# The low parts of one Strassen product first, at another place in SBUF

## The chip, the cores and the metric

The kernel runs on one core of a Trainium2 chip. The metric is the device time of one execution in microseconds, taken as the median of several runs. The times of the engines come from one execution that the hardware profiler recorded.

## What is computed

The reference is one decoder block over 512 positions of 1024 channels, all in float32. What matters here is its last part, the feed-forward layer:

```python
h = rmsnorm(x, norm2_g[l])
gu = h @ w_ffn_in[l]                       # 1024 -> 2 * 2816
g = causal_dwconv(gu[..., :D_FF], ffn_conv_w[l]) + ffn_conv_b[l]
x = x + (jax.nn.silu(g) * gu[..., D_FF:]) @ w_ffn_out[l]
```

Before it come a joint input projection, a gated convolution, an attention with compressed and selected blocks, and their merge. The change does not reach into those.

## The kernel before

**Two parts per number.** Every large product is computed with float32r operands. A float32 value is split into a high part (a rounded copy) and a low part (the rest), and a product is the sum of three: high weights by high data, high weights by low data, low weights by high data. `dense` (from L402) writes this out for a list of units, one unit per 128 input channels: first, for each unit, the two products with the high weights (L405, L406), which load the same weights twice; then, for each unit, the product with the low weights (L408). TensorE runs its matmuls in the order in which the program has them, each with a load of 128 x 128 weights ahead of it.

**The feed-forward layer.** `ff_strassen` (from L992) takes two tiles of 128 output channels at a time, f and f + 1, for f = 0, 2, ... 20. For each it computes two pairs: the gate (n = 0) and the up projection (n = 1). That makes 22 pairs. A pair is a 2 x 2 block product by Strassen's scheme in Winograd's form: 7 products in place of 8. `ff_forms` (from L898) builds the seven weight forms: the blocks a22, a11 and a12 as they are, and four sums of blocks, numbered 1 to 4. `ff_pair` (from L942) runs the seven products into four PSUM banks. Each product has 4 units, so 12 matmuls, with 256 columns of moving data from `xf_h` and `xf_l`; a pair has 84. The first product is always a22 with T4. For f = 0 the gate pair is written differently (`late`, the lines around L969 and L975): its first three units are issued while the data is still being made, and it does not call `dense` for its products.

**Down parts.** Between pairs, `between()` calls `down_part` (from L1013): a share of the last projection. For four tiles f at a time, two of the 8 output tiles are taken, each with 4 units of 512 columns; together 24 matmuls. From about 477 us of the span on, pair and down part take turns in a regular beat. Before that, parts and pairs are interleaved by the scheduler, which orders each engine's instructions with a simulation of the timeline.

**Where the weights lie.** The tiles of the weight forms are taken from the pool `pw` (L831 to L833) and, for a11 and a12, from the ring `wf`:

- `th` and `tl`, the high and the low part of a22, 2048 bytes per partition each, two buffers of each tag;
- `sh` and `sl`, the parts of the sums (three buffers each), `sf`, the sums before the split, and `p1`, all in `pw` behind them;
- `wh` and `wl`, the ring for a11 and a12.

Tiles get their place when their tag is first asked for. The line `pw.tile(..., name="th_", tag="th", bufs=2)` asks for `th` ahead of all others, and `gap_w`, 48 floats that nobody reads, follows it. So `th` begins 288 bytes past a multiple of 512, and `tl`, `sh`, `sl` and all that follow begin at 480. `wh` and `wl` begin at 480 too, and so does everything that the down parts read. The moving tiles `xf_h` and `xf_l` begin at 288. A weight block of one unit is 512 bytes per partition, so every unit of a tile starts at the same place within 512.

**How a22 is filled.** `dma_split` (L157 to L161): ScalarE writes the high part into `th` (L159) and the negated high part into `tl` (L160); then GpSimd issues a transfer that adds the raw weights to `tl` in place (L161). The other forms are split by ScalarE and VectorE (`split`, L152).

Of the kernel before, what the change touches and what calls it, by code (L numbers as in the profile page):

```python
# [11 lines left out]
F32 = mybir.dt.float32  # L12
F32R = mybir.dt.float32r
# [5 lines left out]
P = 128  # L19
D = 1024  # L20
# [62 lines left out]
def tile_block(ctx: ExitStack, tc: tile.TileContext, xT, pos, par, par2, w_tok, w_a3, w_gate, w_ao, w_bo, w_o,  # L83
               w_ff, w_dn, c_w1, out):
    nc = tc.nc
# [10 lines left out]
    def const(shape, name, dt=F32, pool=sb):  # L96
        return pool.tile(shape, dt, name=name, tag=name)
# [14 lines left out]
    def d_bank(name):  # L112
        return bank("d", name, 2)

    def s_bank(name):
        return bank("s", name, 3)

    def t_bank(name):
        return bank("t", name, 2)

    def o_bank(name):
        return bank("o", name, 1)
# [47 lines left out]
    def ring_w(src, name):  # L170
        raw = raw_tile(name)
        nc.sync.dma_start(raw, src)
        h, l = ring(name)
        split(h, l, raw)
        return h, l
# [223 lines left out]
    r1sq = const([P, S], "r1sq", F32, pb)  # L399
    nc.scalar.activation(r1sq, r1b, AF.Square)  # L400

    def dense(acc, units, first=True, last=True):  # L402

        for i, (wh, wl, xh, xl) in enumerate(units):
            nc.tensor.matmul(acc, wh, xh, start=first and i == 0, stop=False)  # L405
            nc.tensor.matmul(acc, wh, xl, start=False, stop=False)  # L406
        for i, (wh, wl, xh, xl) in enumerate(units):
            nc.tensor.matmul(acc, wl, xh, start=False, stop=last and i == len(units) - 1)  # L408

    def w_units(w, xh, xl, nk, k0=0, koff=0):  # L410
        wh, wl = w
        return [(wh[:, (koff + k) * P:(koff + k + 1) * P], wl[:, (koff + k) * P:(koff + k + 1) * P],
                 xh[:, k0 + k, :], xl[:, k0 + k, :]) for k in range(nk)]
# [15 lines left out]
    def compress_in(kv):  # L429
        w = load_w(w_a3[kv], D, f"kc{kv}")  # L430
        acc = d_bank(f"pkc{kv}")
        dense(acc, w_units(w, xg_h, xg_l, KD))
        kc2 = pp.tile([P, 8, G, NU_], F32, name=f"kcb{kv}", tag="kcb", bufs=1)

        pe = pe_sb[:, kv].rearrange("p (n r) -> p r n", r=8)
        for g in range(G):
            nc.gpsimd.tensor_copy(kc2[:, :, g, NC:].rearrange("p r (a n) -> p r a n", a=2),
                                  pe[:, :, None, :].to_broadcast([P, 8, 2, 2]))
            for j in range(2):
                nc.vector.tensor_tensor(  # L440
                    kc2[j * HD:(j + 1) * HD, :, g, 0:NC],
                    acc[g * HD:(g + 1) * HD, :].rearrange("p (n r two) -> p r n two", r=8, two=2)[:, :, :, j],
                    r1b[g * HD:(g + 1) * HD, :].rearrange("p (n r two) -> p r n two", r=8, two=2)[:, :, :, j], op=ALU.mult)
        hi, lo = (kc2s[:, :, i, kv] for i in range(2))
        nc.gpsimd.tensor_copy(hi, kc2)
        nc.vector.tensor_sub(lo, kc2, hi.bitcast(F32))
# [271 lines left out]
    def conv_tile(i):  # L718
        accs = []
        for j in (1, 2, 0):  # L720
            w = load_w(w_a3[2 + 3 * i + j], D, f"a{i}{j}", by="dma" if 3 * i + j > 1 else "vector")
            acc = d_bank(f"pa{i}{j}")
            dense(acc, w_units(w, xg_h, xg_l, KD))
            if j == 1:
                cs_ = f_tile(f"cs{i}")[:, 0:S]
                nc.vector.tensor_mul(cs_, acc, r1sq)
            elif j == 2:
                u = f_tile(f"u{i}")
                nc.gpsimd.memset(u[:, 0:2], 0.0)
                nc.vector.tensor_mul(u[:, 2:], acc, cs_)  # L730
                t = f_tile(f"ct{i}")[:, 0:S]
                causal_conv(t, u, par_sb[:, CAW + 3 * i:CAW + 3 * i + 3])
                nc.gpsimd.tensor_mul(t, t, r1b)
            else:
                nc.vector.tensor_mul(t, acc, t)
                nc.scalar.activation(ya_h[:, i, :], t, AF.Copy)
                nc.vector.tensor_sub(ya_l[:, i, :], t, ya_h[:, i, :].bitcast(F32))
# [3 lines left out]
    def gate_tile(j, t):  # L741
        w = load_w(w_gate[j], D, f"g{j}", by="pool")
        acc = d_bank(f"pg{j}")
        dense(acc, w_units(w, xg_h, xg_l, KD))
        nc.vector.tensor_mul(t, acc, r1b)
        nc.scalar.activation(t, t, AF.Tanh, scale=0.5)
# [57 lines left out]
    for i in range(4):  # L804
# [3 lines left out]
        w = ring_w(w_bo[i], f"bo{i}")  # L808
        for n, j in enumerate((2 * i, 2 * i + 1)):
            acc = t_bank(f"pmb{j}")  # L810
# [18 lines left out]
    xf_h = const([P, 4, 7, TH], "xf_h", F32R, px)  # L829
    xf_l = const([P, 4, 7, TH], "xf_l", F32R, px)  # L830
    pw = ctx.enter_context(tc.tile_pool(name="pw", bufs=1, side="left"))  # L831
    pw.tile([P, D // 2], F32R, name="th_", tag="th", bufs=2)
    const([P, 48], "gap_w", F32, pw)  # L833

    def x_forms(k, v):
        nc.vector.tensor_sub(v[:, T1:T3 + 1], v[:, 1:4:2], v[:, 0:2])
# [5 lines left out]
    for n, j in enumerate(O_ORDER):  # L842
        w = ring_w(w_o[j], f"o{j}")
        acc = d_bank(f"po_{j}")
        units = w_units(w, mix_h, mix_l, KD)
# [96 lines left out]
    def ff_pair(f, n, c, form, late=None):  # L942
        nm = f"{n}_{f}"
        b1, b26 = o_bank(f"p1{nm}"), t_bank(f"p26{nm}")
        b45, b37 = s_bank(f"p45{nm}"), s_bank(f"p37{nm}")
        lo, hi = slice(0, TH), slice(TH, S)

        def units(wf_, x, ks):
            wh, wl = form[wf_]
            return [(wh[:, k * P:(k + 1) * P], wl[:, k * P:(k + 1) * P], xf_h[:, k, x], xf_l[:, k, x]) for k in ks]  # L950

        def product(acc, wf_, x):
            dense(acc, units(wf_, x, range(4)))

        def sums(dst, bank, v):

            nc.vector.tensor_tensor(dst, bank.rearrange("p (a t) -> p a t", a=2), v[:, None, :].to_broadcast([P, 2, TH]),
                                    op=ALU.add)

        p1 = pw.tile([P, TH], F32, name=f"p1{nm}", tag="p1", bufs=1)  # L960
        c1, c2 = c[:, :, 0:TH], c[:, :, TH:]
        plan = [(b26, hi, 2, T2, True), (b37, hi, 3, T3, True), (b37, lo, 4, B22, False), (b45, hi, 1, T1, True),
                (b1, lo, "a11", B11, True), (b26, lo, "a12", B21, False), (b45, lo, "a22", T4, False)]
        if late is not None:

            for b, cols, wf_, x, opens in plan:
                for i, (wh, wl, xh, xl) in enumerate(units(wf_, x, range(3))):
                    for lhs, rhs, st in ((wh, xh, True), (wh, xl, False), (wl, xh, False)):
                        nc.tensor.matmul(b[:, cols], lhs, rhs, start=opens and st and i == 0, stop=False,  # L969
                                         skip_group_check=True)  # L970

            def product(acc, wf_, x):
                (wh, wl, xh, xl), = units(wf_, x, (3,))
                for lhs, rhs, last in ((wh, xh, False), (wh, xl, False), (wl, xh, True)):
                    nc.tensor.matmul(acc, lhs, rhs, start=False, stop=last, skip_group_check=True)  # L975

        product(b45[:, lo], "a22", T4)
        product(b1[:, lo], "a11", B11)
        nc.scalar.activation(p1, b1[:, lo], AF.Copy)
        product(b26[:, lo], "a12", B21)  # L980
        product(b26[:, hi], 2, T2)
        sums(c1, b26, p1)
        product(b37[:, hi], 3, T3)
        product(b37[:, lo], 4, B22)
        sums(c2, b37, c1[:, 1])
        product(b45[:, hi], 1, T1)
        sums(c[:, 1].rearrange("p (a t) -> p a t", a=2), b45, c2[:, 1])
        nc.vector.tensor_add(c2[:, 0], c2[:, 0], b45[:, hi])
# [121 lines left out]
```

## Time and profile before

| | |
|---|---|
| Median of 3 runs | 715.76 us (715.33 to 716.61) |
| The profiled execution: its time | 715.21 us |
| Its span, from the first to the last instruction | 713.5 us |
| Mean granted TensorE clock | 1.00 |
| Matmuls | 4285 |
| HBM read, written | 102.64 MB, 2.10 MB |

The span is shorter than the execution's time by what lies around it. The profile gives, for each engine, its busy time; for each group of equal instructions, the mean duration; and in the timeline, the start of each. A matmul's duration contains the way through the array, so two neighbours overlap: what a matmul costs in a row of matmuls is the distance between two starts, which is less than the duration. Groups in the timeline that are merged (x4) show the start of the first. The weight loads are a row of their own (PEld) and overlap the matmuls.

### The profile page before, as it was taken

The numbers are of one execution on the slowest core, as the hardware profiler recorded it, in microseconds if no ns is written. First come the engines' busy times: TensorE is split into PE (matmuls) and PEld (weight loads), VectorE is DVE, ScalarE is ACT, GpSimd is POOL, SyncE is SP. The second block draws the span as 40 slices with busy tenths as digits, with TensorE's granted clock in tenths as the row PEclk, the third lists the DMA queues.
The fourth block names the chain that finished last, engine by engine and source line by source line (L and its number), as shares of the span: only waits on it lengthen the run. The fifth ranks groups of instructions, "written<-read, shape, count | busy, mean of one in ns | idle before, by whom it ended". The sixth has DMA issues, their size and how long they took to land.

```text
span 713.5 us, 11375 instructions
## 1 busy us (share of the span) xinstructions
PE 708.3 (99%) x4285; PEld 633.5 (89%) x4285; DVE 534.8 (75%) x957; ACT 432.6 (61%) x722; POOL 182.4 (26%) x179
## 2 busy tenths in 40 slices
PE   9999999999999999999999999999999999999997
PEld 9999878888888888888889999899999999999986
DVE  6887886687566878365795899988787877878643
ACT  7535655977667776522676767666555765647440
POOL 4051422133433334433012220221211222111110
PEclk9999999999999999999999999999999999999999
DMA  7333687511121122336386797987978779785565
GB/s 274 97 95 119 172 181 162 135 60 59 60 69 51 60 76 73 118 128 197 94 197 137 174 236 196 226 209 183 213 183 211 175 185 206 185 198 105 123 142 149
DMA packets 41142, 105.47 MB, mean 148 GB/s; under 512 B 3968, under 2 KB 9216, under 8 KB 41088
## 3 DMA queue, kind: packets, MB, share of 16 engines
q1 hardware_dynamic: 26528, 70.41, 30.4%
q0 software_dynamic: 14272, 34.08, 27.6%
q8 instruction: 33, 0.54, 0.3%
q10 hardware_dynamic: 288, 0.26, 0.1%
q14 instruction: 21, 0.17, 0.1%
HBM read 102.64 MB, written 2.10 MB: 147 GB/s over the span
## 4 chain that ended last, share of the span: by engine, by line
PE 96%; DMA 2%; ACT 1%; issue 0%; DVE 0%; POOL 0%; ACTq 0%; POOLq 0%
PE p L406 9%; PE p L405 9%; PE p L408 9%; PE pdn L406 6%; PE pdn L405 6%; PE pdn L408 6%; PE pg L406 4%; PE pg L405 4%; PE pg L408 4%; PE pa L405 2%; PE pt L681 2%; PE pa L406 2%; PE pa L408 2%; PE po L405 2%; PE po L406 2%; PE po L408 2%
## 5 line engine op out<-in xcount | busy, mean ns | idle before, releaser
L406 PE MATMUL p<-xf_l,sh 128*128 128x256 f32 x336 | 80.6, 277 | 0.0
L405 PE MATMUL p<-xf_h,sh 128*128 128x256 f32 x336 | 80.5, 277 | 0.0
L153 ACT ACTIVATE sh<-s 128x1024 fp32r<-128x1024 f32 x44 | 46.2, 1057 | 38.2 <-PE p L406 24.7
L406 PE MATMUL pdn<-al,wh_d 128*128 128x512 f32 x176 | 68.8, 391 | 0.0
L405 PE MATMUL pdn<-ah,wh_d 128*128 128x512 f32 x176 | 68.5, 390 | 0.0
L405 PEld LDWEIGHTS p<-xf_h,sh 128*128 128x128 f32 x336 | 63.0, 188 | 0.1
L406 PEld LDWEIGHTS p<-xf_l,sh 128*128 128x128 f32 x336 | 63.0, 188 | 0.1
L161 POOL DMA_DIRECT2D wl_s<-in_w_ff_dram x22 | 19.5, 885 | 167.2 <-ACT wl_s L160 155.9
L154 DVE TENSOR_TENSOR sl<-s,sh 128x1024 fp32r<-128x1024 f32 x44 | 53.8, 1224 | 8.7 <-ACT sh L153 8.7
L159 ACT ACTIVATE wh_s<-wr_s 128x1024 fp32r<-128x1024 f32 x22 | 23.3, 1059 | 53.1 <-PE pdn L406 50.1
L408 PE MATMUL p<-xf_h,sl 128*128 128x256 f32 x336 | 51.5, 277 | 0.0
L136 POOL TENSOR_TENSOR wl_g<-wr_g,wh_g 128x1024 fp32r<-128x1024 f32 x16 | 38.4, 2401 | 50.7 <-ACT wh_g L134 25.4
L405 PE MATMUL pg<-xg_h,wh_g 128*128 128x512 f32 x128 | 50.7, 396 | 0.0
L406 PE MATMUL pg<-xg_l,wh_g 128*128 128x512 f32 x128 | 50.6, 395 | 0.0
L408 PE MATMUL pdn<-ah,wl_d 128*128 128x512 f32 x176 | 47.7, 389 | 0.0
L161 POOL DMA_DIRECT2D wl_d<-in_w_dn_dram x22 | 26.5, 1203 | 77.2 <-ACT wl_d L160 69.0
L1029 DVE TENSOR_TENSOR x<-x,pdn 128x512 f32<-128x512 f32 x48 | 33.0, 688 | 16.2 <-PE pdn L408 15.5
L408 PEld LDWEIGHTS p<-xf_h,sl 128*128 128x128 f32 x336 | 44.6, 188 | 0.2
L405 PE MATMUL p<-xf_h,wh_s 128*128 128x256 f32 x168 | 40.5, 276 | 0.0
L406 PE MATMUL p<-xf_l,wh_s 128*128 128x256 f32 x168 | 40.5, 276 | 0.0
L408 PEld LDWEIGHTS pdn<-ah,wl_d 128*128 128x128 f32 x176 | 33.0, 188 | 6.9
L406 PEld LDWEIGHTS pdn<-al,wh_d 128*128 128x128 f32 x176 | 33.0, 188 | 6.2
(359 smaller groups left out, 2123.1 us busy)
## 6 DMA issues: line engine op xcount, KB each, us to landing
wr_s<-in_w_ff_dram SPq DMA_DIRECT2D x44, 512.0 KB, 4.9
wl_s<-in_w_ff_dram POOLq DMA_DIRECT2D x22, 512.0 KB, 7.2
wr_d<-in_w_dn_dram SPq DMA_DIRECT2D x22, 512.0 KB, 7.0
wl_d<-in_w_dn_dram POOLq DMA_DIRECT2D x22, 512.0 KB, 8.2
wr_g<-in_w_gate_dram SPq DMA_DIRECT2D x16, 512.0 KB, 3.4
wr_a<-in_w_a_dram SPq DMA_DIRECT2D x12, 512.0 KB, 4.1
tl<-in_w_ff_dram POOLq DMA_DIRECT2D x22, 256.0 KB, 6.9
wl_a<-in_w_a_dram POOLq DMA_DIRECT2D x10, 512.0 KB, 7.9
```

Source lines behind the costliest of these rows:

```text
L136: e.tensor_sub(lo[:, 0:n], raw[:, 0:n], hi[:, 0:n].bitcast(F32))
L153: hi = nc.scalar.activation(h, v, AF.Copy)
L154: nc.vector.tensor_sub(l, v, h.bitcast(F32))
L159: nc.scalar.activation(h, raw, AF.Copy)
L161: nc.gpsimd.dma_start(l if dst is None else dst, src, accum_op=ALU.add)
L405: nc.tensor.matmul(acc, wh, xh, start=first and i == 0, stop=False)
L406: nc.tensor.matmul(acc, wh, xl, start=False, stop=False)
L408: nc.tensor.matmul(acc, wl, xh, start=False, stop=last and i == len(units) - 1)
L681: nc.tensor.transpose(pt[:, i * P:(i + 1) * P], e[:, i, (kt + k0) * P:(kt + k0 + 1) * P], ident)
L1029: nc.vector.tensor_add(xj, xj, acc)
```

## The change

`dense` gets an argument `low_first`. With it, the products with the low weights are issued ahead of those with the high ones; without it the order is as before. `ff_pair` sets it for the a22 product alone. In the pool `pw`, `tl` is now asked for ahead of the others, with a gap of 80 floats ahead of it and one of 96 floats behind it in place of 48; `th` gets its place behind that gap, where its tag is first asked for. So `tl` begins 96 bytes past a multiple of 512, and `th` at 480; all others keep their place within 512 and lie 512 bytes further on. The gate pair of f = 0 keeps its order, and has its tiles at the new places.

```diff
-    def dense(acc, units, first=True, last=True):
-
-        for i, (wh, wl, xh, xl) in enumerate(units):
-            nc.tensor.matmul(acc, wh, xh, start=first and i == 0, stop=False)
-            nc.tensor.matmul(acc, wh, xl, start=False, stop=False)
-        for i, (wh, wl, xh, xl) in enumerate(units):
-            nc.tensor.matmul(acc, wl, xh, start=False, stop=last and i == len(units) - 1)
+    def dense(acc, units, first=True, last=True, low_first=False):
+
+        products = [(wl, xh) for wh, wl, xh, xl in units]
+        highs = [(wh, x) for wh, wl, xh, xl in units for x in (xh, xl)]
+        products = products + highs if low_first else highs + products
+        for i, (w, x) in enumerate(products):
+            nc.tensor.matmul(acc, w, x, start=first and i == 0, stop=last and i == len(products) - 1)
...
     pw = ctx.enter_context(tc.tile_pool(name="pw", bufs=1, side="left"))
-    pw.tile([P, D // 2], F32R, name="th_", tag="th", bufs=2)
-    const([P, 48], "gap_w", F32, pw)
+
+    const([P, 80], "gap_v", F32, pw)
+    pw.tile([P, D // 2], F32R, name="tl_", tag="tl", bufs=2)
+    const([P, 96], "gap_w", F32, pw)
...
         def product(acc, wf_, x):
-            dense(acc, units(wf_, x, range(4)))
+            dense(acc, units(wf_, x, range(4)), low_first=wf_ == "a22")
```

## The prediction

> **What bounds the kernel.** I read the page from the top: the busy shares, the granted clock, then the chain that ended last.
>
> ```profile
> PE 708.3 (99%) x4285; PEld 633.5 (89%) x4285; DVE 534.8 (75%) x957; ACT 432.6 (61%) x722; POOL 182.4 (26%) x179
> PEclk9999999999999999999999999999999999999999
> PE 96%; DMA 2%; ACT 1%; issue 0%; DVE 0%; POOL 0%; ACTq 0%; POOLq 0%
> ```
>
> TensorE is busy 99% of the span at the full granted clock, and 96% of the chain that ended last is its own work. So only two things can move the time here: the distance from one matmul's start to the next one's, which I call the step, and a wait put in front of a matmul. The matmuls themselves stay the same in number and size, 12 for each a22 product.
>
> Next, the groups by line and shape, from 477 us to 693 us, where pairs and down parts alternate regularly (columns: line, engine, operation, output<-inputs, shapes, count | busy us, mean ns | idle before).
>
> ```profile
> L405 PE MATMUL p<-xf_h,sh 128*128 128x256 f32 x224 | 53.5, 276 | 0.0
> L406 PE MATMUL p<-xf_l,th 128*128 128x256 f32 x56 | 13.9, 282 | 0.0
> L405 PE MATMUL p<-xf_h,th 128*128 128x256 f32 x56 | 13.9, 281 | 0.0
> L408 PE MATMUL p<-xf_h,tl 128*128 128x256 f32 x56 | 8.6, 276 | 0.0
> ```
>
> All four rows are one shape, 256 columns. Only those whose weights lie in th, the high parts of a22, last 281 to 282 ns in place of 276. By the sizes in the code th is the one weight tile that does not start at 480 bytes past a multiple of 512: gap_w is 48 floats, so th lies 192 bytes lower than the rest, at 288. What a duration means for the step is read from the starts in the timeline. First an a22 product straight behind another pair:
>
> ```profile
> 406.84 0.28 PE L405 MATMUL p<-xf_h,th 128*128 128x256 f32 x1
> 406.96 0.28 PE L406 MATMUL p<-xf_l,th 128*128 128x256 f32 x1
> ...
> 407.80 0.28 PE L408 MATMUL p<-xf_h,tl 128*128 128x256 f32 x1
> ```
>
> Eight matmuls in 407.80 - 406.84 = 0.96 us: a step of 120 ns. Now one behind a down part, with the rest of its pair, up to the next down part:
>
> ```profile
> 491.67 1.07 PE L408 MATMUL pdn<-ah,wl_d 128*128 128x512 f32 x4
> 492.58 0.28 PE L405 MATMUL p<-xf_h,th 128*128 128x256 f32 x1
> ...
> 493.53 0.62 PE L408 MATMUL p<-xf_h,tl 128*128 128x256 f32 x4
> ...
> 502.14 0.39 PE L405 MATMUL pdn<-ah,wh_d 128*128 128x512 f32 x1
> ```
>
> From 492.58 to 493.53 the eight th matmuls take 0.95 us, 119 ns each. The other 76 of the pair (4 of tl, six products of 12) take 502.14 - 493.53 = 8.61 us, 113.3 ns each. The third place is the one that matters most. Here a down part was sorted into the a22 product, so that only one th matmul stands between the 512-column work and the rest of the pair:
>
> ```profile
> 462.34 0.84 PE L408 MATMUL pdn<-ah,wl_d 128*128 128x512 f32 x3
> 463.02 0.28 PE L406 MATMUL p<-xf_l,th 128*128 128x256 f32 x1
> 463.14 0.63 PE L408 MATMUL p<-xf_h,tl 128*128 128x256 f32 x4
> 463.61 0.28 PE L405 MATMUL p<-xf_h,wh_s 128*128 128x256 f32 x1
> ...
> 472.09 0.39 PE L405 MATMUL pdn<-ah,wh_d 128*128 128x512 f32 x1
> ```
>
> The same 76 matmuls, same weights' places, same moving tiles, take 472.09 - 463.14 = 8.95 us, 117.8 ns each. So TensorE has two rates for the same 256-column work, a short step of 113.3 ns and a long one of 117.8 ns, and keeps the one it has fallen into until something disturbs it. The next place shows what can disturb it:
>
> ```profile
> 396.57 1.10 PE L408 MATMUL p<-xf_h,sl 128*128 128x256 f32 x8
> 397.52 0.28 PE L405 MATMUL p<-xf_h,th 128*128 128x256 f32 x1
> ...
> 398.23 0.62 PE L408 MATMUL p<-xf_h,tl 128*128 128x256 f32 x4
> 398.68 0.28 PE L405 MATMUL p<-xf_h,wh_s 128*128 128x256 f32 x1
> ```
>
> Before the six th matmuls the step is long (397.52 - 396.57 = 0.95 for eight, 119 ns); after them it is short (398.68 - 398.23 = 0.45 for four, 113 ns). The reading I go by: th, out of line with the rest, costs some 6 ns a matmul, and in return a run of it brings TensorE from the long step back to the short one. A single th does not (463.02); six or eight do.
>
> **The change, part by part.** The order of the 12 matmuls becomes 4 of tl, then 8 of th. gap_v adds 80 floats (320 bytes) ahead of tl: 288 + 320 = 608, that is 96 past 512. gap_w grows to 96 floats, so th and all behind it begin at 288 + 704 = 992, which is 480 past 512. All other tiles move by 512 bytes and keep their place within 512.
>
> *High parts.* Eight th matmuls now have weights placed as all others are. If the short step holds, they take 8 x 113.3 = 907 ns. Now they take 950 behind a down part and 960 behind a pair. That takes off 43 ns or 53 ns.
>
> *Low parts.* Four tl matmuls move from 480 to 96. No row shows weights at 96. From below: they cost nothing more than now, 113.3 ns; no group of this shape has a shorter settled step, and I see no reason for one. From above: the settled step of th, 120 ns, 4 x 6.7 = 27 ns more. I take 11 ns, nearer to the low end, since behind a down part the full price isn't reached at once (119 against 120 ns). So 32 ns go per product behind a down part, 42 behind a pair.
>
> *How many.* The 22 products divide so: those behind a down part run from 492.58 to the last one,
>
> ```profile
> 671.99 1.07 PE L408 MATMUL pdn<-ah,wl_d 128*128 128x512 f32 x4
> 672.90 0.28 PE L405 MATMUL p<-xf_h,th 128*128 128x256 f32 x1
> ```
>
> With 15.03 us for 84 short steps and 24 of 512 columns (492.58 to the th of the next pair at 507.61), that is 13 of them, and one before at 477.55: 14 x 32 = 0.45 us. Two stand behind a pair, as at 406.84: 2 x 42 = 0.08 us. Six lie in the stretch from 380 to 477 us, mixed with other work; I give them 0 to 50 ns each, 0.1 us in all. Sum: about 0.6 us less. Against the profiled execution (715.21 us, of which 713.5 are the span and 1.7 lie around it) that is 714.6; the median of the runs is 0.55 us above that execution, so 715.76 - 0.6 = **715.2 us**.
>
> *The wait.* With its low parts first, a22 needs tl 0.95 us earlier. Tl comes through a transfer that GpSimd issues and that adds in place:
>
> ```profile
> 507.61 0.28 PE L405 MATMUL p<-xf_h,th 128*128 128x256 f32 x1
> 496.64 0.85 POOL L161 DMA_DIRECT2D tl<-in_w_ff_dram x1
> DMA to landing us min/median/max: 3.9/6.9/9.4
> ```
>
> The issue at 496.64 lands at the latest 9.4 us on, at 506.0, and the next a22 product begins at 507.61. Even if it were for that product, 1.6 us would be left; with two buffers per tile it is more likely meant for the one behind. So the wait is hidden, under the pair's and the down part's own matmuls. Without that cover TensorE would stand for up to 0.95 us per pair, with nothing else queued to go ahead of tl. DVE, ACT, GpSimd and SyncE get no instruction more, and none is moved on their queues.
>
> *A rule that speaks against it.* The row: th 281 to 282 ns, the others 276, and where the weights start is what the code sets apart. The Trainium skill, page "SBUF — State Buffer", section "Who interferes with whom", has TensorE read its moving operand and its weights through two independent ports and never wait on anyone, so the start within 512 bytes would be of no account and the change worth nothing. The trace disagrees as far as these rows go.
>
> **Rivals.** *The low parts at 96 do not restore the short step.* This is the one on the slow side. After 512-column work the place at 463.02 kept the long step for a whole pair, with weights at 480. If four matmuls at 96 are too few, or if 96 acts as 480 does, each of the 14 pairs behind a down part runs all its 84 matmuls at 117.8 ns: 9.89 us in place of 0.95 + 8.61 = 9.56, 0.33 us more. 14 x 0.33 = 4.6 us: 720.4 us. It decides in the first four steps of a pair. For it: the th run behind a down part needs more than one matmul, I have seen six and eight work, and 4 is half of what is there now. Against it: the moving tiles xf_h and xf_l begin at 288, so 480 lies 192 bytes ahead of them and 96 lies 192 bytes behind; th, right at their place, restores slowly, and a third place may do it sooner.
>
> *Place is of no account.* Then th is slow for what it is (its product, its bank, being first) and the change moves only the order: 715.8, give or take 0.2. For it: all th's lie in the pair's first product. Against it: the tl of that product has 276 ns.
>
> *The stretch from 380 to 477 us falls out otherwise.* There pairs and parts are interleaved and the long step is common:
>
> ```profile
> L405 PE MATMUL p<-xf_h,sh 128*128 128x256 f32 x112 | 27.0, 278 | 0.0
> ...
> L405 PE MATMUL p<-xf_h,sh 128*128 128x256 f32 x16 | 3.9, 279 | 0.0
> ```
>
> The first row is that stretch, 278 ns in the mean; the second is the long-step pair from 463.5 to 472.5 us alone, 279; the short step has 276. A pair that changes sides there is worth 0.34 us (76 x 4.5 ns). Three gained beside the forecast's 0.6: 714.2 us. Three lost: 716.2, which is within what counts as no change.
>
> **Chances.** A measurement of this kernel can tell about 0.2%, 1.4 us, from no change. The forecast, with its own range from 714.4 to 716.2 (a loss in the early stretch included): 0.52. Place of no account: 0.08. Both are within 0.2%: 0.60. The low parts fail to restore: 0.30. A gain past 1.4 us through the early stretch: 0.10. Faster 0.10, same 0.60, slower 0.30. Since the failing case has more than 2 in 10, the range must reach it: 714.2 to 720.8 us.
>
> **What would show it.** Right: the th groups at 276 ns, eight th in 0.91 us, the pair behind a down part still 8.6 us for 76 matmuls, and sh, sl and wh_s at 276 ns from 477 us on. If tl at 96 acts as th did, its groups show 280 to 282 ns. Wrong by the first rival: sh, sl and wh_s at 279 ns for whole pairs and 15.3 us instead of 15.03 from pair to pair. Wrong by the second: tl now has the 282 ns although th has 276, or th keeps 282 at its new place. A wait would show as idle time in front of the tl matmuls with GpSimd's transfer as its end.

## The result, and the profile after

| | before | after |
|---|---|---|
| Median of 4 runs each, side by side | 716.02 us (715.33 to 716.61) | 721.13 us (720.25 to 721.46) |
| Ratio after / before, 95% interval | | 1.0074 (1.0061 to 1.0086) |
| The profiled execution, its span | 715.21 us, 713.5 us | 720.25 us, 718.5 us |

The change costs 5.1 us, 0.7%. That is not the forecast of 715.2 us but its first rival, priced at 720.4; 721.13 us lies 0.3 us above even the upper end of the range, 720.8. The page of the kernel after, in the lines that were read of before (busy shares, clock, chain):

```profile
PE 713.2 (99%) x4285; PEld 637.9 (89%) x4285; DVE 534.8 (74%) x957; ACT 432.6 (60%) x722; POOL 182.2 (25%) x179
PEclk9999999999999999999999999999999999999999
PE 97%; DMA 2%; ACT 0%; DVE 0%; issue 0%; ACTq 0%
```

TensorE has as many matmuls as before, the same clock, and is the chain by itself. It is busy 4.9 us longer (713.2 against 708.3), nearly all of the 5.0 us by which the span grew. So nobody waits for anything new; the same matmuls follow each other more slowly. Which ones, the groups by line and shape from 477 to 698 us tell:

```profile
L408 PE MATMUL p<-xf_h,sh 128*128 128x256 f32 x224 | 55.2, 279 | 0.0
...
L408 PE MATMUL p<-xf_h,th 128*128 128x256 f32 x56 | 13.8, 279 | 0.0
...
L408 PE MATMUL p<-xf_h,tl 128*128 128x256 f32 x56 | 8.9, 282 | 0.0
```

th, now at 480, is no longer out of line: 279 ns, like sh. But sh, which keeps its place within 512 bytes, went from 276 to 279 ns, the mark of the long step, and so did all the rest of the pairs. The last column is the idle time ahead of the group: 0.0 ahead of tl, so the wait for its transfer is hidden. Now the starts in the timeline, from one down part over a pair to the next pair:

```profile
476.84 1.08 PE L408 MATMUL pdn<-ah,wl_d 128*128 128x512 f32 x4
477.75 0.64 PE L408 MATMUL p<-xf_h,tl 128*128 128x256 f32 x4
478.23 0.28 PE L408 MATMUL p<-xf_h,th 128*128 128x256 f32 x1
...
479.17 0.28 PE L408 MATMUL p<-xf_h,wh_s 128*128 128x256 f32 x1
...
487.65 0.39 PE L408 MATMUL pdn<-ah,wh_d 128*128 128x512 f32 x1
...
493.12 0.64 PE L408 MATMUL p<-xf_h,tl 128*128 128x256 f32 x4
```

The four tl steps take 478.23 - 477.75 = 0.48 us, 120 ns each, and the eight of th 0.94, 117.5 each. The long step stays to the end: th and all behind it, 80 matmuls, take 487.65 - 478.23 = 9.42 us, 117.8 ns each. The whole pair is 9.90 us, the down part 5.47 as before. From pair to pair it is 15.37 us in place of 15.03 (15.374 and 15.027 before rounding). Fourteen times 0.347 us is 4.9 us: nearly all of the loss is here.

Behind another pair, where the short step was already running, nothing of the kind happens:

```profile
406.98 0.62 PE L408 MATMUL p<-xf_h,tl 128*128 128x256 f32 x4
407.43 0.28 PE L408 MATMUL p<-xf_h,th 128*128 128x256 f32 x1
...
408.34 0.28 PE L408 MATMUL p<-xf_h,wh_s 128*128 128x256 f32 x1
```

Four tl at 96 in 0.45 us and eight th in 0.91: 113 ns each, so here 96 costs nothing. And at a place in the early stretch the four even end a long step:

```profile
395.26 0.28 PE L408 MATMUL p<-xf_l,sh 128*128 128x256 f32 x1
...
396.55 0.62 PE L408 MATMUL p<-xf_h,tl 128*128 128x256 f32 x4
397.01 1.07 PE L408 MATMUL p<-xf_h,sl 128*128 128x256 f32 x8
397.91 0.28 PE L408 MATMUL p<-xf_h,th 128*128 128x256 f32 x1
```

Ahead of them 11 matmuls (by the count of rows) take 396.55 - 395.26 = 1.29 us, 117 ns each; behind them 8 take 0.90 us, 113 ns. So "four at 96 can't restore the short step" would be too much said. What they fail at is the long step behind a down part.

### The profile page after: what moved, and what is told of

The parts are those of the page before. It is cut to its first block, busy times and chain, and to the rows that moved or that the text cites. A ratio compares the mean times of both kernels' runs of the same rounds, so it can differ in the third digit from the quotient of the medians.

```text
span 718.5 us, 11361 instructions
## 1 busy us (share of the span) xinstructions
PE 713.2 (99%) x4285; PEld 637.9 (89%) x4285; DVE 534.8 (74%) x957; ACT 432.6 (60%) x722; POOL 182.2 (25%) x179
## 4 chain that ended last, share of the span: by engine, by line
PE 97%; DMA 2%; ACT 0%; DVE 0%; issue 0%; ACTq 0%
PE p L408 29%; PE pdn L408 17%; PE pg L408 12%; PE pa L408 8%; PE po L408 6%; PE pma L408 3%; PE pmb L408 3%; PE pt L681 2%; PE pj_s L255 2%; PE pj_s L257 2%; PE pj_s L256 2%; PE pkc L408 2%; PE po L692 1%; PE po L687 1%; PE sc L602 1%; PE sc L603 1%
## 5 line engine op out<-in xcount | busy, mean ns | idle before, releaser
L408 PE MATMUL p<-xf_l,sh 128*128 128x256 f32 x336 | 82.7, 279 | 0.0
L408 PE MATMUL p<-xf_h,sh 128*128 128x256 f32 x336 | 82.4, 279 | 0.0
L408 PEld LDWEIGHTS pdn<-ah,wh_d 128*128 128x128 f32 x176 | 33.0, 188 | 6.4
```

What stands on the lines that cost most here:

```text
L408: nc.tensor.matmul(acc, w, x, start=first and i == 0, stop=last and i == len(products) - 1)
```

## The experiments

The change has two halves, the places and the order, and the expectations name theories by short words. **Order**: the low parts in front are what costs. **Place**: weights at 96 don't end the long step behind a down part. **Number**: four matmuls out of line are too few, eight are enough. Later: **Alignment**: the long step comes about because the down parts read their moving data (ah, al) at 480 and the pairs theirs (xf_h, xf_l) at 288. **Width**: it comes about by the turn from 512 to 256 columns, wherever the data lie. Each ratio is against the kernel before, run on the same chip beside it.

**1. The places alone.** Against the changed kernel; the high parts go first again, now at 480, the low parts behind them at 96.

```diff
-            dense(acc, units(wf_, x, range(4)), low_first=wf_ == "a22")
+            dense(acc, units(wf_, x, range(4)), low_first=False)
```

> High parts first again, tl at 96 and th at 480 as in the changed kernel. Theory Order (issuing the low parts first is what costs): about 716.0 us, 15.03 us from pair to pair. Theories Place (weights at 96 do not end the long step that 512-column work leaves) and Number (four matmuls are too few): the eight high parts at 480 begin the pair in the long step, and all hangs on whether the four low parts at 96 end it once it has settled; if they do, about 716.5 us and 15.03 to 15.06 us from pair to pair, if not, about 721 us and 15.37.

720.6 us against 715.8: 1.0067 (1.0050 to 1.0085), from pair to pair 15.37 us. The long step stays although the order is that of before, so the order is not needed for the loss. The four tl at 96 stand eight matmuls behind the down part here, and the long step outlasts them too: the eight wh_s behind them take 0.94 us.

**2. The order alone.** Against the changed kernel; th back at 288, tl at 480, low parts first.

```diff
-    const([P, 80], "gap_v", F32, pw)
-    pw.tile([P, D // 2], F32R, name="tl_", tag="tl", bufs=2)
-    const([P, 96], "gap_w", F32, pw)
+    pw.tile([P, D // 2], F32R, name="th_", tag="th", bufs=2)
+    const([P, 48], "gap_w", F32, pw)
```

> Low parts first, but at the places of the kernel before: tl at 480, th at 288. Theory Order: about 721 us. Theories Place and Number: the four low parts run in the long step, the eight high parts at 288 then end it as before, so 716.0 to 716.5 us, and 15.03 to 15.05 us from pair to pair; all later products of a pair at 276 ns.

720.92 us against 715.8 (one of its four runs took 724.98): 1.0085 (1.0056 to 1.0113). This missed what the theories Place and Number expected: eight matmuls at 288 are there as before, and the loss is there all the same. Its timeline behind a down part, and then at a place without one:

```profile
429.03 0.63 PE L408 MATMUL p<-xf_h,tl 128*128 128x256 f32 x4
429.50 0.28 PE L408 MATMUL p<-xf_h,th 128*128 128x256 f32 x1
...
430.46 0.28 PE L408 MATMUL p<-xf_l,wh_s 128*128 128x256 f32 x1
430.57 0.62 PE L408 MATMUL p<-xf_h,wl_s 128*128 128x256 f32 x4
...
432.38 0.28 PE L408 MATMUL p<-xf_h,sh 128*128 128x256 f32 x1
...
477.05 1.07 PE L408 MATMUL pdn<-ah,wl_d 128*128 128x512 f32 x4
477.95 0.64 PE L408 MATMUL p<-xf_h,tl 128*128 128x256 f32 x4
478.43 0.28 PE L408 MATMUL p<-xf_h,th 128*128 128x256 f32 x1
...
479.38 0.28 PE L408 MATMUL p<-xf_h,wh_s 128*128 128x256 f32 x1
...
480.32 0.63 PE L408 MATMUL p<-xf_h,wl_s 128*128 128x256 f32 x4
```

At 429.50, out of a long step (tl: 0.47 us for four), the eight th take 0.96 us, the settled 120 ns, and behind them the step is short: 16 matmuls from 430.57 to 432.38, 113 ns each. Behind the down part the four tl come first, 0.48 us; then the same eight th take 0.95, and the next eight still 0.94, 117.5 ns. So whether a run out of line ends the long step hangs on the start it gets, not on its place and number alone. Either half of the change is enough to lose the 5 us. (The four tl have a mean of 282 ns in this run, with weights at 480.)

**3. The low parts first, at 288.** Against the changed kernel; th and all else at 480.

```diff
-    const([P, 80], "gap_v", F32, pw)
     pw.tile([P, D // 2], F32R, name="tl_", tag="tl", bufs=2)
-    const([P, 96], "gap_w", F32, pw)
+    const([P, 48], "gap_w", F32, pw)
```

> Low parts first, with tl at 288 and th at 480: four matmuls at the place where eight worked. Theory Number: four are too few, about 721 us and 15.37 us from pair to pair. Theory Place: 288 ends the long step, 96 does not, so about 715.6 us and 15.00 us from pair to pair.

722.18 us against 715.8: 1.0087 (1.0072 to 1.0102).

```profile
478.52 0.63 PE L408 MATMUL p<-xf_h,tl 128*128 128x256 f32 x4
479.00 0.28 PE L408 MATMUL p<-xf_h,th 128*128 128x256 f32 x1
479.11 0.28 PE L408 MATMUL p<-xf_l,th 128*128 128x256 f32 x1
...
479.94 0.28 PE L408 MATMUL p<-xf_h,wh_s 128*128 128x256 f32 x1
```

One step is short (479.11 - 479.00), then the seven to 479.94 have 118 ns again. Four right behind a down part are too few even at 288, the place that works with eight.

**4. The high parts at 96.** Against the kernel before; its order, th at 96 in place of 288, all else at 480.

```diff
+    const([P, 80], "gap_v", F32, pw)
     pw.tile([P, D // 2], F32R, name="th_", tag="th", bufs=2)
-    const([P, 48], "gap_w", F32, pw)
+    const([P, 96], "gap_w", F32, pw)
```

> High parts first, eight of them at 96, tl and the rest at 480. Theory Number (four were too few): eight at 96 end the long step as eight at 288 do, about 716 us, 15.03 us from pair to pair. Theory Place (96 does not do it behind a down part): about 721 us, 15.37 to 15.40 us.

720.86 us against 715.51: 1.0075 (1.0061 to 1.0088), 15.37 us from pair to pair. Eight at 96 fail where eight at 288 succeed. So the low parts at 96 would not have been saved by being eight: with the data where they lie here, 96 is the wrong place behind a down part.

**5. Nothing out of line.** Against the kernel before; all weights at 480.

```diff
-    pw.tile([P, D // 2], F32R, name="th_", tag="th", bufs=2)
     const([P, 48], "gap_w", F32, pw)
```

> High parts first, with th, tl and everything else at 480: nothing stands out of line. Theories Place and Number: the long step that 512-column work leaves stays for each whole pair, about 721 us and 15.37 us from pair to pair, th at 279 to 280 ns as all others. Theory Order, or if 288 only cost time: no matmul is dearer than another, about 715.2 us and 15.00 us.

721.31 us against 715.8: 1.0080 (1.0065 to 1.0095). Its groups from 477 to 693 us:

```profile
L405 PE MATMUL p<-xf_h,sh 128*128 128x256 f32 x224 | 55.3, 280 | 0.0
...
L405 PE MATMUL p<-xf_h,th 128*128 128x256 f32 x56 | 13.9, 281 | 0.0
```

No matmul differs from the kernel before except by the place of th's weights, and the whole pair is long. That makes th at 288 worth 5.5 us to the kernel before, for the 0.04 to 0.05 us that it costs per pair.

**6. Two matmuls at 288.** Against the kernel before; everything at 480 except a copy of th's first unit at 288, which serves the first two matmuls. ScalarE makes one copy more per pair.

```diff
-    pw.tile([P, D // 2], F32R, name="th_", tag="th", bufs=2)
+    pw.tile([P, P], F32R, name="t0_", tag="t0", bufs=1)
...
+        t0 = pw.tile([P, P], F32R, name=f"t0{nm}", tag="t0", bufs=1)
+        nc.scalar.activation(t0, a22[:, 0:P], AF.Copy)
+        form["t0"] = t0
...
-            dense(acc, units(wf_, x, range(4)))
+            us = units(wf_, x, range(4))
+            if wf_ == "a22":
+                us[0] = (form["t0"],) + us[0][1:]
+            dense(acc, us)
```

> Everything at 480 but a copy of the high part's first unit, at 288, that serves the first two matmuls of a pair (one ScalarE copy of 128 columns more for each pair). Theory Number: two are too few, about 721 us and 15.37 us from pair to pair. Rival (the first matmul at 288 already brings the start back in step, and the others of the eight only cost): about 715.4 us and 14.99 us.

721.47 us against 715.51: 1.0084 (1.0070 to 1.0098), 15.36 us from pair to pair. Two are too few.

**7. The down parts' data at 288.** Against experiment 5, in which nothing is out of line and every pair is long. ah and al lie below the gap in their pool, which ends at the upper end of SBUF; 48 floats behind them move them, and them alone, from 480 to 288, where xf_h and xf_l are.

```diff
     a_tiles(0)
+    const([P, 48], "gap_a", F32, pf)
```

> All weights at 480, nothing out of line, high parts first, as in the kernel with everything at 480; but the down parts' moving tiles ah and al begin at 288, as the pairs' moving tiles xf_h and xf_l do. Theory Alignment (the long step comes of going from moving tiles at 480 to moving tiles at 288, and matmuls of 512 columns hide their weight loads): the down part hands over in the short step, 84 x 113.3 + 24 x 226.7 ns = 14.96 us from pair to pair, 714 to 715.3 us. Theory Width (going from 512 columns to 256 does it, wherever the data lies): about 721 us, 15.37 us.

715.92 us (715.15 to 716.61) against 715.51: 1.0004 (0.9995 to 1.0013). That is 0.6 us above what Alignment expected at most, but the 5.5 us of experiment 5 are gone, without any weight out of line. First the timeline of experiment 5 behind a down part, then that of experiment 7:

```profile
478.34 1.07 PE L408 MATMUL pdn<-ah,wl_d 128*128 128x512 f32 x4
479.25 0.28 PE L405 MATMUL p<-xf_h,th 128*128 128x256 f32 x1
...
480.19 0.63 PE L408 MATMUL p<-xf_h,tl 128*128 128x256 f32 x4
480.66 0.28 PE L405 MATMUL p<-xf_h,wh_s 128*128 128x256 f32 x1
```

```profile
475.25 1.08 PE L408 MATMUL pdn<-ah,wl_d 128*128 128x512 f32 x4
476.17 0.39 PE L405 MATMUL pdn<-ah,wh_d 128*128 128x512 f32 x1
...
478.00 1.08 PE L408 MATMUL pdn<-ah,wl_d 128*128 128x512 f32 x4
478.92 0.28 PE L405 MATMUL p<-xf_h,th 128*128 128x256 f32 x1
...
479.83 0.62 PE L408 MATMUL p<-xf_h,tl 128*128 128x256 f32 x4
480.28 0.28 PE L405 MATMUL p<-xf_h,wh_s 128*128 128x256 f32 x1
```

Eight th: 0.94 us there, 0.91 here. The pair has the short step from its first matmul on, with nothing to restore it; in its groups sh has 276 ns. The turn to 256 columns is still there, so Width falls, and Alignment forecast the right step for the pairs behind whole down parts. But it isn't free: the 12 matmuls of 512 columns from 476.17 to 478.92 take 2.75 us, 229 ns each, and no longer 226.7. Over the 24 of a down part that is some 53 ns, so from pair to pair it takes 15.01 us, and not the 14.96 that 84 short steps of 113.3 ns and 24 of 226.7 would give. And in the early stretch, where no th at 288 ends a long step any more, the step is long: sh has 279 ns in the groups from 385 to 436 us, against 277 before.

The two traces show there that Alignment is not the whole rule. At the same point of the program, two matmuls of a down part stand alone among those of a pair, first in experiment 5 (data at 480), then in experiment 7 (data at 288):

```profile
426.84 0.28 PE L405 MATMUL p<-xf_h,sh 128*128 128x256 f32 x1
...
427.90 0.39 PE L406 MATMUL pdn<-al,wh_d 128*128 128x512 f32 x1
...
428.35 1.07 PE L408 MATMUL p<-xf_h,sl 128*128 128x256 f32 x8
429.26 0.39 PE L406 MATMUL pdn<-al,wh_d 128*128 128x512 f32 x1
```

```profile
427.08 0.28 PE L405 MATMUL p<-xf_h,sh 128*128 128x256 f32 x1
...
428.10 0.39 PE L406 MATMUL pdn<-al,wh_d 128*128 128x512 f32 x1
...
428.56 1.11 PE L408 MATMUL p<-xf_h,sl 128*128 128x256 f32 x8
429.50 0.39 PE L406 MATMUL pdn<-al,wh_d 128*128 128x512 f32 x1
```

The nine sh ahead of the two take 1.06 us in experiment 5, 118 ns each, and 1.02 us in experiment 7, 113 ns. The eight sl behind them take 0.91 us in experiment 5, 113 ns each, and 0.94 us in experiment 7, 118 ns. So with the data at 480 the two end the long step, with nothing out of line, and with the data at 288 they start it. That is the reverse of what whole down parts do, so the number of 512-column matmuls in a row matters too. In the traces of all runs, every row of 12 or 24 of them leaves the long step with the data at 480 and the short one with the data at 288 or 32. Rows of two leave the short step in 8 of 12 cases with the data at 480, and the long one in all four with the data at 288 or 32. Why the length matters was not tested.

**8 and 9. The change with the down parts' data moved.** Against the changed kernel: the same line with 48 floats (ah, al at 288), and with 112 (at 32).

```diff
     a_tiles(0)
+    const([P, 48], "gap_a", F32, pf)
```

> The changed kernel (low parts first, tl at 96, th at 480), with the down parts' moving tiles ah and al at 288 as in the run before this. Theory Alignment: the pairs begin in the short step, where four low parts at 96 cost nothing (113 ns each in the changed kernel's trace, behind a pair in the short step), so 15.01 us from pair to pair as in the run with all weights at 480; and in the stretch before the regular beat 96 sometimes ends a long step, which nothing did in that run: 714.8 to 715.9 us. If 96 is itself what upsets the start of a pair behind 512 columns: about 721 us, 15.37 us from pair to pair.

> The same with ah and al at 32 past a multiple of 512, that is 256 bytes from 288. If what counts is the place within 256 bytes: as the kernel with 288, 15.01 us from pair to pair, the down part's matmuls at 226 to 231 ns in turn, 714.8 to 715.9 us. If it is the place within 512 bytes: another hand-over, most likely the long step again, about 720 us, 15.3 to 15.4 us from pair to pair.

At 288: 714.88 us (714.22 to 718.62) against 715.27, 1.000 (0.9991 to 1.0010). At 32: 715.78 us against 715.27, 1.0013 (1.0001 to 1.0025). The loss is gone in both. (At 32 the runs spread from 714.50 to 719.18.) Groups with data at 288, from 477 to 690 us, then the timeline behind a down part:

```profile
L408 PE MATMUL p<-xf_h,sh 128*128 128x256 f32 x224 | 53.5, 276 | 0.0
...
L408 PE MATMUL p<-xf_h,tl 128*128 128x256 f32 x56 | 8.8, 279 | 0.0
```

```profile
476.61 1.08 PE L408 MATMUL pdn<-ah,wl_d 128*128 128x512 f32 x4
477.53 0.63 PE L408 MATMUL p<-xf_h,tl 128*128 128x256 f32 x4
478.00 0.28 PE L408 MATMUL p<-xf_h,th 128*128 128x256 f32 x1
...
478.90 0.28 PE L408 MATMUL p<-xf_h,wh_s 128*128 128x256 f32 x1
```

The same tl at 96, the same order, and now four are done in 0.47 us and the step behind them is short (th: 0.90 us for eight). With the data at 32, sh and tl have the same means, 276 and 279 ns, and the same 15.03 us from pair to pair: in this case places 256 bytes apart act alike. No run has the data anywhere else than at 480, 288 and 32, so two readings stay: that the data must lie where the pairs' data lie, to within 256 bytes, or only that they must not lie at 480, where the weights are. Neither kernel is faster than the one before: with the data at 288 the pair takes 9.53 us in place of 9.56, and the down part's 229 ns give that back.

A next step would be to move the weights too, so that they begin where all the moving data begin. It was not tried.

## Why the prediction was wrong

**The bound, right.** Only the step and a wait could move the time; the change came as step, with TensorE at 99% and the clock at its full.

**The wait at nothing, right.** No idle time stands ahead of tl.

**The high parts at 480, right in size.** th lost its extra 6 ns: its duration is now that of sh, and 113 ns is its step wherever the step is short (406.98, and experiment 8). The working put "if the short step holds" ahead of it. It didn't hold.

**The low parts at 96, the failing step.** The working counted 11 ns for the four tl together and let them do the work of restoring that eight th had done. As a price, 11 ns was fair: 0 behind a pair, some 12 ns in experiment 8 (0.465 us for four, against 0.453). What failed is the restoring behind a down part: it doesn't happen, and the 84 matmuls pay some 4.5 ns each, 0.37 us per pair beside the forecast. The runs show that to mend one condition alone would not have helped: at 96 eight would not do it either (experiment 4), four would not do it at 288 either (3), and eight at 288 don't do it once four others come first (2). The prediction knew two conditions, place and number; there is a third, the start that the run gets. It also took a run of th for what brings the short step back; two matmuls of a down part can do it too (428.35 in experiment 5). Its one argument against the rival, that a third place might restore sooner than th's, was drawn from the distance to xf_h and was not borne out with ah and al at 480.

**The rival's price, right.** 9.89 us for the long pair against 9.90 measured; 0.33 us per pair against 0.35, of which about 0.01 is the down part's own, most of it in its last step (233 ns ahead of tl at 96, against 226); 4.6 us against 5.0 in the span.

**"Place is of no account", fell.** Experiment 5 moves one tile's weights and nothing else, and costs 5.5 us; experiment 7 moves the down parts' data by 192 bytes and takes it back. The sign that the prediction gave for this rival (tl with 282 ns) did show, most likely for another reason: tl is now first behind the 512 columns, and has 282 ns there at 480 too (experiment 2). That sign could not tell the two apart; the 279 ns of sh could.

**The early stretch, of no weight.** sh has 277 ns from 385 to 436 us in both kernels, and the pairs behind the down parts account for 4.9 of the 5.0 us.

**The rule that was weighed.** The Trainium skill, page "SBUF — State Buffer", section "Who interferes with whom", has TensorE's two read ports independent and never waiting. Experiments 5 and 7 differ by where two moving tiles lie, and the same matmuls on other tiles, xf_h with th or sh, go from 117.8 to 113.3 ns. So the place of what TensorE read before matters here; whether the two reads hold each other up is not shown by that.

**What stays open.** Why there are two steps at all, and what the down part leaves behind that keeps the long one. Why 96 ends a long step at 396.55 us, but not behind a down part with the data at 480. Why the number of 512-column matmuls in a row matters. The runs show when it happens and what it costs, not the part of the chip that does it.

## What to carry to other kernels

When one group of matmuls looks slow for no reason, ask before it is repaired what the groups behind it would do without it: th's extra 6 ns on eight matmuls kept 76 others at 113.3 ns. Read the rate of a row of matmuls from starts, not durations, and in the stretch right behind a change of shape. Where a rate sticks, a place to try is the start of the work ahead of it: here, moving the down parts' data brought the pairs back to 113.3 ns without any tile out of line. It did so behind rows of 12 and 24 and not behind rows of two, and it made the moved work itself slower (229 ns for 226.7), so a pair and a down part were no faster together than in the kernel before.

## What was not expected of the hardware

- 256-column matmuls of the same shape and clock have two steps, 113.3 and 117.8 ns, and keep one of them for 80 matmuls on end (9.42 us at 117.8).
- A moving tile's place acts beyond its own matmuls: ah and al at 480 or 288 decide the step of matmuls that read xf_h and xf_l behind a down part (experiments 5 and 7, 720.0 and 714.9 us of span).
- The same move makes the 512-column matmuls slower, 229 ns for 226.7.
- Two 512-column matmuls in a row turn the step round: from 118 to 113 ns with their data at 480 (428.35 us in experiment 5), from 113 to 118 with their data at 288 (428.56 us in experiment 7).
- The same eight weights at 288 end the long step from one start (429.50 us in experiment 2) and not from another (478.43 us in the same trace).
